# Row copies of a roll in HBM: two DMA rings over the same blocks, or over two halves of the rows

## The chip, the cores and the metric

The kernel runs on one core of one Trainium2 chip. The metric is the device time of one execution in microseconds (us). Times of a kernel are given as the median of several runs with their lowest and highest; a profile is of one execution.

## The reference

A matrix of 8192 x 8192 float32 (256 MiB) is rolled by 100 columns along its rows:

```python
def setup_inputs():
    return {"x": np.random.randn(8192, 8192).astype(np.float32), "shift": 100}

def reference(x, shift):
    return np.roll(x, shift, axis=1)
```

So `out[r, c] = x[r, c - 100]`, and the last 100 columns of x come round to the first 100 of out. Nothing is computed: the kernel moves 268.44 MB from one tensor in HBM to another.

## The kernel before

With n_cols = 8192 and shift 100, `s` is 100, `a` is s rounded up to a multiple of 128, that is 128, and `g = a - s` is 28. Each output row falls into two parts.

The body, columns `a` to 8191 of out, is columns `g` to 8091 of x: 8,064 elements or 32,256 bytes of each row, copied from HBM to HBM with nothing between (lines 31 to 36). `xm` and `om` (lines 31 and 32) view the rows as blocks `c` of 64 rows, each as 16 groups `e` of 4 rows `j`. One DMA takes a fixed `c` and `j` and all 16 `e`: 16 rows, 4 rows (128 KiB) apart. A DMA of 16 rows is spread over 16 DMA engines, one row on each. The loops run over 128 blocks and four `j`; `engines[j % 2]` gives j = 0 and 2 to the queue of SP and j = 1 and 3 to that of ACT, so both queues walk through the same blocks at the same time, on neighbouring rows (32 KiB apart). Each queue issues 256 DMAs. The framework hands out eight completion semaphores to the DMAs of the two queues in turn, four for each queue, and before a DMA reuses a semaphore its queue waits until the DMA that had it has landed. So at most four copies of each queue are under way.

The head, columns 0 to 127 of out, goes through on-chip memory (lines 53 to 75). It is issued by POOL, on a third queue: ten loads into the tiles `t` and `h` (lines 64 to 70; two stages `k` of 4,096 rows), four copies on VectorE that join the pieces from `t` into `h` (lines 68 and 71), and eight stores of 512 bytes per row (line 75). It writes other columns than the body and neither waits for it nor is waited for.

Line 36 is the only line of the body that issues anything:

```python
    if a < n_cols:
        for c in range(n_rows // 64):
            for j in range(4):
                engines[j % 2].dma_start(out=om[c, j, :, a:], in_=xm[c, j, :, g:n_cols - s])
```

Lines 37 to 47 serve other shifts and issue nothing here.

Of the kernel before, what the change touches and what calls it, by code (L numbers as in the profile page):

```python
# [1 line left out]

# [4 lines left out]


@with_exitstack
def kernel(  # L10
    ctx: ExitStack,
    tc: tile.TileContext,
    x: bass.AP,
    shift: int,
    out: bass.AP,
):
    nc = tc.nc
    n_rows, n_cols = x.shape
    s = shift % n_cols
    a = -(-s // 128) * 128  # L20
    g = a - s
    P = nc.NUM_PARTITIONS
    engines = [nc.sync, nc.scalar]
    n_chunks = 16
    rows = n_rows // n_chunks

    xm = x.rearrange("(c e j) w -> c j e w", e=16, j=4)
    om = out.rearrange("(c e j) w -> c j e w", e=16, j=4)
    if a < n_cols:
        for c in range(n_rows // 64):
            for j in range(4):
                engines[j % 2].dma_start(out=om[c, j, :, a:], in_=xm[c, j, :, g:n_cols - s])
    if a == 0:
        return


    if a > 512:
        for i in range(n_chunks):
            r = slice(i * rows, (i + 1) * rows)
            nc.gpsimd.dma_start(out=out[r, :s], in_=x[r, n_cols - s:])
            if g > 0:
                nc.gpsimd.dma_start(out=out[r, s:a], in_=x[r, :g])
        return

    Q, J = 4, 8
    n_st = n_rows // (P * Q * J)
    reads = ctx.enter_context(tc.tile_pool(name="reads", bufs=n_st))
    heads = ctx.enter_context(tc.tile_pool(name="heads", bufs=n_st))
    xt = x.rearrange("(k p j q) c -> k q p j c", q=Q, j=J, p=P)
    ot = out.rearrange("(k p j q) c -> k q p j c", q=Q, j=J, p=P)
    tiles = []
    for k in range(n_st):  # L60
        t = reads.tile([P, Q - 1, J, a], x.dtype)
        h = heads.tile([P, Q, J, a], x.dtype)
        for q in range(1, Q):
            lead = bass.AP(tensor=x.tensor, offset=(k * P * J * Q + q) * n_cols - s,
                           ap=[[J * Q * n_cols, P], [Q * n_cols, J], [1, a]])
            nc.gpsimd.dma_start(out=t[:, q - 1], in_=lead)  # L66
        nc.gpsimd.dma_start(out=h[:, Q - 1, :, :s], in_=xt[k, Q - 1, :, :, n_cols - s:])  # L67
        nc.vector.tensor_copy(h[:, :Q - 1, :, :s], t[:, :, :, :s])  # L68
        if g > 0:
            nc.gpsimd.dma_start(out=h[:, 0, :, s:], in_=xt[k, 0, :, :, :g])  # L70
            nc.vector.tensor_copy(h[:, 1:, :, s:], t[:, :, :, s:])  # L71
        tiles.append(h)
    for k, h in enumerate(tiles):
        for q in range(Q):
            nc.gpsimd.dma_start(out=ot[k, q, :, :, :a], in_=h[:, q])  # L75


# [1 line left out]
_INS = ['x', 'shift']  # L79
_OUTS = [((8192, 8192), 'float32')]  # L80

_NUMBERS = {'shift': 100}


# [26 lines left out]
```

## Time and profile before

| What | Value |
|---|---|
| median of 6 runs | 829.52 us (828.35 to 831.01) |
| the profiled execution | 830.07 us |
| its span, first to last instruction | 828.3 us |
| VectorE busy | 3.7 us |
| POOL busy | 16.1 us |
| POOL's stores (line 75), issue to landing, median | 97.5 us |
| one DMA issue on SP / ACT (line 36), median | 0.510 / 0.517 us |
| first and last issue of line 36 on SP | 0.7 / 815.1 us |

The profile cuts the span into 40 equal slices of 20.7 us and gives for each the mean busy share of the 16 DMA engines in tenths and the GB/s that they moved. A byte that goes from HBM to HBM is counted once in these GB/s, and twice (read and written) in the line on HBM. A line of the queues gives packets, MB and the time that the packets took as a share of what 16 engines had in the span; "software" is POOL's queue, "hardware" those of SP and ACT. A line of the issues gives output and input, the queue, the number of DMAs, KB each and the median us from issue to landing.

### The profile page before, as it was taken

What the parts mean: (1) busy time and instruction counts of PE and PEld (TensorE: products, weight loads), DVE (VectorE), ACT (ScalarE), POOL (GpSimd) and SP (SyncE); (2) the same over time, 40 slices, a digit from 0 to 9 for tenths busy, and PEclk for the clock granted to TensorE, in tenths of its full rate; (3) what the DMA queues carried; (4) which work ended last, traced back from release to release, by engine and by line L of the source; (5) the groups of instructions that cost most, each with busy time, mean ns of one, the idle gap of its engine ahead of it and who ended that gap; (6) DMA issues with size and microseconds to landing.
All of it is one profiled execution on the core that took longest, in us unless ns stands there. A gap on an engine that the chain in (4) does not pass through costs nothing. (4 is left out here: it accounts for less than half of the span.)

```text
span 828.3 us, 589 instructions
## 1 busy us (share of the span) xinstructions
DVE 3.7 (0%) x4; POOL 16.1 (2%) x22
## 2 busy tenths in 40 slices
DVE  0000000000000000000000000000000000000000
POOL 3001001000000000000000000000000000000000
DMA  9999999999999999999999999999999999999998
GB/s 296 324 338 340 339 335 352 344 337 352 345 336 336 326 322 327 327 326 330 321 332 327 335 329 324 327 332 321 324 338 316 334 337 322 329 330 329 333 326 271
DMA packets 18724, 272.70 MB, mean 329 GB/s; under 512 B 8480, under 2 KB 8480, under 8 KB 10528
## 3 DMA queue, kind: packets, MB, share of 16 engines
q1 hardware_dynamic: 8192, 132.14, 47.9%
q10 hardware_dynamic: 8192, 132.14, 47.2%
q0 software_dynamic: 2336, 8.39, 3.9%
q14 instruction: 4, 0.03, 0.0%
HBM read 268.44 MB, written 268.44 MB: 648 GB/s over the span
## 5 line engine op out<-in xcount | busy, mean ns | idle before, releaser
L75 POOL DMA_DIRECT2D out_dram<-h x8 | 6.9, 957 | 92.4 <-DMA h<-in_x_dram 81.2
L66 POOL DMA_DIRECT2D t<-in_x_dram x6 | 5.4, 912 | 0.8 <-PEq L106 0.8
L68 DVE COPY h<-t 128x2400 f32<-128x2400 f32 x2 | 2.8, 1410 | 117.5 <-DMA t<-in_x_dram 117.5
L67 POOL DMA_DIRECT2D h<-in_x_dram x2 | 1.8, 884 | 16.5 <-DMA t<-in_x_dram 16.5
L70 POOL DMA_DIRECT2D h<-in_x_dram x2 | 1.8, 884 | 13.6 <-DMA t<-in_x_dram 13.6
L71 DVE COPY h<-t 128x672 f32<-128x672 f32 x2 | 1.0, 504 | 0.0
L92 POOL MEMSET const-float32-0.0<- 128x1 f32 x1 | 0.1, 100 | 0.2 <-issue 0.2
L92 POOL MEMSET const-bfloat16-1.0<- 128x1 bf16 x1 | 0.1, 103 | 0.0
L92 POOL MEMSET const-float32-1.0<- 128x1 f32 x1 | 0.1, 100 | 0.0
L92 POOL MEMSET const-uint8-127<- 128x1 uint8 x1 | 0.1, 100 | 0.0
## 6 DMA issues: line engine op xcount, KB each, us to landing
out_dram<-in_x_dram ACTq DMA_DIRECT2D x256, 504.0 KB, 12.7
out_dram<-in_x_dram SPq DMA_DIRECT2D x256, 504.0 KB, 12.7
out_dram<-h POOLq DMA_DIRECT2D x8, 512.0 KB, 97.5
t<-in_x_dram POOLq DMA_DIRECT2D x6, 512.0 KB, 67.8
h<-in_x_dram POOLq DMA_DIRECT2D x2, 400.0 KB, 85.1
h<-in_x_dram POOLq DMA_DIRECT2D x2, 112.0 KB, 82.7
```

What stands on the lines that cost most here:

```text
L66: nc.gpsimd.dma_start(out=t[:, q - 1], in_=lead)
L67: nc.gpsimd.dma_start(out=h[:, Q - 1, :, :s], in_=xt[k, Q - 1, :, :, n_cols - s:])
L68: nc.vector.tensor_copy(h[:, :Q - 1, :, :s], t[:, :, :, :s])
L70: nc.gpsimd.dma_start(out=h[:, 0, :, s:], in_=xt[k, 0, :, :, :g])
L71: nc.vector.tensor_copy(h[:, 1:, :, s:], t[:, :, :, s:])
L75: nc.gpsimd.dma_start(out=ot[k, q, :, :, :a], in_=h[:, q])
L92: nc = _bacc.Bacc("TRN2", target_bir_lowering=False, num_devices=1)
```

## The change

The body's loop runs over half as many blocks, and in each step issues two DMAs: SP copies row `j` of each group of block `c`, ACT the same of block `c + 64`. SP goes through rows 0 to 4095 and ACT through rows 4096 to 8191. Each queue issues 256 DMAs of 16 rows, in the order SP, ACT, SP, ACT; the shape of a DMA, the bytes and the rest of the kernel stay.

```diff
     if a < n_cols:
-        for c in range(n_rows // 64):
+        half = n_rows // 64 // 2
+        for c in range(half):
             for j in range(4):
-                engines[j % 2].dma_start(out=om[c, j, :, a:], in_=xm[c, j, :, g:n_cols - s])
+                for q, eng in enumerate(engines):
+                    eng.dma_start(out=om[q * half + c, j, :, a:], in_=xm[q * half + c, j, :, g:n_cols - s])
```

## The prediction

> **What bounds the kernel now.** I read the page of the profiled execution first: its span, the slices, the queues and the HBM line.
>
> ```profile
> span 828.3 us, 589 instructions
> ...
> DMA  9999999999999999999999999999999999999998
> GB/s 296 324 338 340 339 335 352 344 337 352 345 336 336 326 322 327 327 326 330 321 332 327 335 329 324 327 332 321 324 338 316 334 337 322 329 330 329 333 326 271
> DMA packets 18724, 272.70 MB, mean 329 GB/s; under 512 B 8480, under 2 KB 8480, under 8 KB 10528
> ...
> q1 hardware_dynamic: 8192, 132.14, 47.9%
> q10 hardware_dynamic: 8192, 132.14, 47.2%
> q0 software_dynamic: 2336, 8.39, 3.9%
> ...
> HBM read 268.44 MB, written 268.44 MB: 648 GB/s over the span
> ```
>
> The reader is to see that the 16 DMA engines are busy from the first slice to the last, nearly all of it with the two hardware rings (q1 and q10, those of SP and ACT), and that the engine's other work (POOL's queue, q0) takes 3.9%. Each ring has 8,192 packets: 4,096 rows of 32,256 bytes (132.14 MB / 4,096) and as many 4-byte completion writes. So each engine carries 8,192 / 16 = 512 rows.
>
> Next, the issues and the waits of the queues, to see whether issuing limits anything.
>
> ```profile
> out_dram<-in_x_dram ACTq DMA_DIRECT2D x256, 504.0 KB, 12.7
> out_dram<-in_x_dram SPq DMA_DIRECT2D x256, 504.0 KB, 12.7
> ```
>
> ```profile
> SPq L36 <- DMA out_dram<-in_x_dram: 679.7, 252, 3.9
> ```
>
> SP issued 256 copies and before 252 of them it waited for an older copy to land, 679.7 us in all: four copies are in flight per ring, and the queue idles for lack of landings, not the other way round. An issue takes 0.51 us (the records of line 36), so 256 of them need 131 us of 828. The count agrees: 8 copies in flight x 516,096 bytes / 12.7 us = 325 GB/s, the rate of the slices. The chain of waits is of no use here: it follows POOL and stops 139 us into the span, while the end is set by the last row copies, issued at 815 us.
>
> Last, the stretch in which the two rings are alone (POOL's last packet starts at about 256 us; the stretch is 289.9 to 807.6 us, slices 15 to 39).
>
> ```profile
> DMA packets 10530, 169.77 MB, mean 328 GB/s; under 512 B 5266, under 2 KB 5266, under 8 KB 5266
> ...
> q1 hardware_dynamic: 5266, 84.94, 51.1%
> q10 hardware_dynamic: 5262, 84.81, 48.6%
> ```
>
> Half of the 10,528 ring packets are rows: 5,264 rows in 517.7 us on 16 engines, 1,574 ns for each row and its completion write (9 ns by the packet records). The records of single packets show what those 1,574 ns are made of. The shortest row took 1,192 ns (27.1 GB/s on one engine), 1,579 of the 8,192 rows took under 1,200 ns, the median is 1,485, the mean 1,529, and one in ten is over 1,941. The floor is so sharp that I read it as an engine's own pace, and the excess, 1,529 - 1,192 = 337 ns a row, as waiting for memory that 16 engines read and write at once. That the floor is the engine's and the excess the memory's is inference; that excess exists is read off.
>
> **The change, part by part.** The sum before, per engine: rings 47.9% + 47.2% = 95.1% of 828.3 = 787.7 us; POOL's queue 3.9% = 32.3 us; together 820.0 us; the other 8.3 us are the edges (the first and last slices, 296 and 271 GB/s) and gaps. Around the span lie 830.07 - 828.3 = 1.8 us. The profiled execution's 830.07 us is 0.55 above the median of 829.52, so I add differences to the median.
>
> Copies issued: 256 on SP and 256 on ACT, each 16 rows by 8,064 elements, before and after. Removed 0, added 0. The built program has the same rows of instructions on every engine, the same four copies in flight per ring, and the waits stand before the same copies. Price 0, since count and durations (0.51 us per issue, hidden under 679.7 us of waiting) don't change; if that cover were gone the issue would still need only 131 us beside 788 us of transfers. POOL's 18 DMAs and VectorE's four copies (3.7 us) are untouched; they had 550 us to spare before, so a later landing of theirs delays nothing. No wait is added.
>
> What moves is which row a ring is at. Before, one engine meets rows 4e, 4e+1, 4e+2, 4e+3 of a block by turns from the two rings: 32 KiB apart, all in one 128 KiB piece, and the 16 engines walk a window of a few MiB together. After, the SP ring gives it row 4e + j of block c, and the ACT ring row 4e + j of block c + 64: 4,096 rows, exactly 128 MiB, further. Both windows are then walked at once, in x and in out. The trace of before shows no pair of row copies that far apart, so its cost is bounded from rows nearby.
>
> The near rows are the slices with the rings alone, in which relative positions of the 16 engines drift: mean 327.9 GB/s, slowest 316, fastest 338. If all ring time ran at the slowest, 787.7 x (327.9/316 - 1) = +29.7 us; at the fastest, 787.7 x (327.9/338 - 1) = -23.5 us. The far row is the excess itself: doubled, 512 x 337 ns = +173 us; gone, -173 us. A gain near that far end I exclude, because these bytes would then pass at 537 / 655 us = 820 GB/s, while no slice of this execution with rings alone moved above 2 x 338 = 676 GB/s to and from HBM.
>
> I take a loss and put it halfway between no effect and the slowest slice: 29.7 / 2 = +14.9 us, so 829.5 + 14.9 = **844 us**. The reason for the sign: an engine overlaps the write of one row with the read of the next (inference: the rows follow each other back to back while their writes need to land). Before, these two rows are neighbours, 32 KiB apart in their tensors; after, they sit at the same place in windows a power of two apart, where the same banks of memory are likelier to be asked for two different lines. The reason for a small size: only one of an engine's neighbours changes, whereas the 16 engines still stand on 16 different rows, 128 KiB apart. It is nearer to the slices than to the doubled excess, since the rings alternate on one engine and never run in step side by side.
>
> A rule of the Trainium skill speaks against this change. In the trace, POOL's descriptors, which step far through x among the ring rows in the first 250 us, don't harm these: the third slice to the thirteenth read 335 to 352 GB/s, POOL's own bytes included. DMA: Bandwidth & Descriptors, "Latency and other measured facts", tells that copies whose partitions lie megabytes apart at a power of two lose up to half their rate (pitch of 512 KiB 207 GB/s, of 4 MiB 103). By that rule at its worst the ring time would double, to some 1,600 us; by the trace's POOL rows it would not move. I take neither as it stands: the page's streams run in step on many partitions, and POOL's pieces are 512 bytes.
>
> A second page bounds a gain. The trace's HBM line shows 648 GB/s. HBM Reference, "Specifications (TRN2)", gives about 716 GB/s per domain; by it the sum could not fall below 537 MB / 716 GB/s = 750 us, an estimate.
>
> **The rivals.**
>
> *No difference.* The rings' addresses don't matter because 16 engines, drifted against each other, already spread over the memory, and the rate is a ceiling of read and write traffic together. For it: slices with the rings alone stay within 4% of 328 for 500 us whatever the engines' drift, and each engine does the same work. Against it: one row takes from 1,192 to over 1,941 ns, so something in the pattern decides. It gives 829.5 us, and it includes the case that the change does not do what it says: the instruction stream is the same, so if memory places both halves alike nothing is left of it.
>
> *Faster, through less crowding.* One mechanism: at present all 16 engines and both rings stand in one window of a few MiB, and rows of neighbouring addresses queue for the same lines of memory; two windows spread them. Its place is the excess of 337 ns a row. For it: only one row in five runs at the floor. Against it: the two rings have to share the same memory rate afterwards, and slices above 335 are rare. At the fastest slice's rate it gives 829.5 - 23.5 = 806 us, at half of that gain 818 us. It decides from where the gain in waiting, per row, passes what the 128 MiB pairing costs (15 us / 512 = 29 ns by my figure); with less than that my forecast's sign stands.
>
> *Strong aliasing.* The windows fall on the same banks and the excess rises by over a third. A third is 512 x 112 ns = +57.5 us, 887 us; doubled it is 829.5 + 173 = 1,002 us. For it: the distance is an exact power of two in both tensors. Against it: x and out, equal in size, are probably placed a whole tensor apart, so such pairs of a read and a write exist already.
>
> **How the numbers follow.** Slower by up to a third of the excess: 0.48, and 844 us as its value. Strong aliasing: 0.10. No difference (within 0.2%, 1.7 us, which is what a measurement of this kernel can tell): 0.12. Faster: 0.30. So faster 0.30, same 0.12, slower 0.58. The range runs from the fastest slice's 806 us to the 888 us where strong aliasing begins; beyond lie that rival's 0.10 and, below, some 0.06 of the faster case. The likeliest case's own range is 831.5 to 888.
>
> **What would show it.** If I am right: the slices with the rings alone fall to about 322 GB/s in the mean (327.9 x 787.7 / 802.6), the DMA row stays at 9 throughout, the landing time of a copy rises from 12.7 to about 12.9 us, fewer rows take under 1,200 ns, the SP queue's wait rises by about the 15 us that the span grows, and POOL's busy time is unchanged. If the faster rival holds: slices of 333 to 338, landing near 12.4 us, more rows at the floor. If there is no difference, mean and spread of the slices stay. I would be wrong in the step on issue if a DMA slice fell below 9 in the middle, or if the SP queue's wait fell by more than the span; wrong in the sign if the mean row took under 1,529 ns; and wrong in size alone if the rate dropped below 305 GB/s with busy engines.

## The result and the profile after

The changed kernel takes 833.3 us in the median of 16 runs (830.0 to 835.01), the kernel before 829.31 us in 35 runs beside it (826.34 to 831.54): a ratio of 1.0047, 95% interval 1.0036 to 1.0057, or 3.9 us more (829.31 x 0.0047). The sign is the forecast's; the size is a quarter of the forecast 14.9 us.

The page of the changed kernel, in the order of the lines shown of before (span, slices, queues, HBM, issues):

```profile
span 829.8 us, 589 instructions
...
DMA  9999999999999999999999999999999999999997
GB/s 298 345 342 332 327 344 349 331 344 353 345 349 321 327 334 327 333 325 330 327 331 331 316 328 323 325 330 325 333 325 328 327 327 327 337 328 327 323 320 252
...
q10 hardware_dynamic: 8192, 132.14, 48.1%
q1 hardware_dynamic: 8192, 132.14, 46.9%
q0 software_dynamic: 2336, 8.39, 4.0%
...
HBM read 268.44 MB, written 268.44 MB: 647 GB/s over the span
...
out_dram<-in_x_dram ACTq DMA_DIRECT2D x256, 504.0 KB, 12.8
out_dram<-in_x_dram SPq DMA_DIRECT2D x256, 504.0 KB, 12.8
```

The reader is to see that nothing has changed its kind: the same packets, the same number of issues, DMA engines busy throughout. The rings' shares make (48.1% + 46.9%) x 829.8 = 788.3 us an engine, against 787.7 before; POOL's 33.2 against 32.3; the rest 8.3 in both. This profiled execution took 831.54 us, the second shortest of the 16, and the one of before 830.07, so between the two pages stand 1.5 of the 3.9 us, and a share rounded to a tenth of a per cent is good to 0.4 us. The waits of SP's queue and the stretch with the rings alone (289.9 to 807.6 us) of the changed kernel:

```profile
SPq L39 <- DMA out_dram<-in_x_dram: 681.7, 252, 4.7
```

```profile
DMA packets 10513, 169.51 MB, mean 327 GB/s; under 512 B 5257, under 2 KB 5257, under 8 KB 5257
...
q10 hardware_dynamic: 5254, 84.78, 50.1%
q1 hardware_dynamic: 5257, 84.71, 49.5%
```

SP waits 2.0 us longer for landings, and 10,511 ring packets fit where 10,528 did. Both point to slower rows; but in two single executions that differ by less than the runs of one kernel do (830.0 to 835.0), they can't carry an explanation. What follows rests on ratios from repeated runs.

### The profile page after: what moved, and what is told of

Its sections match the earlier page's. It is cut to its first block, busy times and chain, and to the rows that moved or that the text cites. A ratio compares the mean times of both kernels' runs of the same rounds, so it can differ in the third digit from the quotient of the medians.

```text
span 829.8 us, 589 instructions
## 1 busy us (share of the span) xinstructions
DVE 3.7 (0%) x4; POOL 16.1 (2%) x22
## 2 busy tenths in 40 slices
DMA packets 18724, 272.70 MB, mean 329 GB/s; under 512 B 8480, under 2 KB 8480, under 8 KB 10528
## 3 DMA queue, kind: packets, MB, share of 16 engines
q10 hardware_dynamic: 8192, 132.14, 48.1%
q1 hardware_dynamic: 8192, 132.14, 46.9%
## 6 DMA issues: line engine op xcount, KB each, us to landing
out_dram<-in_x_dram ACTq DMA_DIRECT2D x256, 504.0 KB, 12.8
out_dram<-in_x_dram SPq DMA_DIRECT2D x256, 504.0 KB, 12.8
```

## The experiments

All of them move all rows with 512 copies of 16 rows, and what is changed is which row follows which. Where a kernel changes something else as well (which rows one copy takes, which queue issues it, where the rows are written), the text says so. "Row number" means j, the place of a row in its group of four, each row 32 KiB after the one before. One ring's rows and the other's come to an engine by turns: a row of each ring, then both completion writes. The packet records don't name the engine, but their times show it: with the rings alone, 92% of ACT's rows in the kernel before and 84% in the changed kernel start within 5 ns of the end of a row of SP, and 96% and 95% of SP's rows within 5 ns of the end of a completion write of ACT. So an order can be written as the row numbers that one engine meets: before 0 1 2 3, after 0 0 1 1 2 2 3 3. Ratios are to the kernel before on the same chip; that kernel took 820.4 to 821.2 us in the first four groups (on three chips) and 828.8 us in the last one (on a fourth), so times are compared inside a group only. The ratios are not quotients of the medians given beside them, and lie up to 0.0016 above or 0.0007 below these.

### Distance or row number

The changed kernel again, with the block and the row of a copy named `b` and `r` (after_again); the edits below are against it where nothing else is said:

> The changed kernel once more, as the measure for its neighbours on the same chip. All theories: 1.0047 of the kernel before, within 0.001.

Measured 1.0058 (1.0045 to 1.0071), 824.33 us against 820.39.

With ACT's rows turned by two (half_rows_turned):

```diff
-                    b, r = q * half + c, j
+                    b, r = q * half + c, (j + 2 * q) % 4
```

> As the changed kernel, but ACT takes the four rows of a group in the order 2, 3, 0, 1, so the two rings stand 128 MiB plus or minus 64 KiB apart. Theory A (the exact power of two makes the two rings' rows ask for the same banks; 64 KiB is enough to leave them): about 1.000, 829 us. Theory B (two windows far apart cost, whatever their exact distance): 1.0047, 833 us.

Measured 1.0004 (0.9994 to 1.0013): the loss is gone, with the rings still 128 MiB apart, give or take 64 KiB.

With ACT's blocks turned (half_blocks_turned):

```diff
-                    b, r = q * half + c, j
+                    b, r = q * half + (c + 21 * q) % half, j
```

> As the changed kernel, but ACT begins its half 21 blocks further on and comes round to them at the end: 170 MiB, later 42 MiB apart, no power of two. Theory A with banks chosen by higher bits of the address: about 1.000, 829 us. Theory B: 1.0047, 833 us.

Measured 1.0091 (1.0076 to 1.0106). No power of two in the distance, and no less loss.

SP the even blocks, ACT the odd ones (alternate_blocks):

```diff
-                    b, r = q * half + c, j
+                    b, r = 2 * c + q, j
```

> SP copies the even blocks and ACT the odd ones, all four rows of each: the rings stand 2 MiB apart, in one window. Theory B: about 1.000, 829 us, since the window stays one. Theory C (not the distance, but that an engine no longer gets neighbouring rows from the two rings in turn): 1.0047, 833 us. Theory A: between the two, as 2 MiB is a power of two as well.

Measured 1.0084 (1.0068 to 1.01). The rings are 2 MiB apart, in one window, and the loss is there. So theory B falls by two of these kernels, and theory A's large power of two by half_blocks_turned. Theory C, that an engine needs neighbouring rows from the two rings, falls by half_rows_turned, whose order 0 2 1 3 has none. Against after_again (up to 1.0071), the two kernels with the larger loss differ by some 0.3%; the interval of alternate_blocks overlaps its own, that of half_blocks_turned (from 1.0076) does not. That part isn't explained.

The same turn in the near arrangement (alternate_blocks_turned, against alternate_blocks):

```diff
-                    b, r = 2 * c + q, j
+                    b, r = 2 * c + q, (j + 2 * q) % 4
```

> SP the even blocks, ACT the odd ones, 2 MiB apart, but ACT takes the four rows of a group in the order 2, 3, 0, 1. Theory D (what costs is that the two rings are at the same row number j of their groups of four, that is, at addresses that agree in the bits of 32 and 64 KiB; distance is of no account): 1.000, against 1.0084 without the turn. Theory B (distance): 1.008 again.

Measured 1.0011 (0.9996 to 1.0026). At 2 MiB as at 128 MiB the loss comes and goes with the row numbers alone. The traces show it in the stretch with the rings alone (289.9 to 807.6 us); first alternate_blocks:

```profile
q10 hardware_dynamic: 5275, 85.10, 52.5%
q1 hardware_dynamic: 5273, 85.07, 47.2%
```

and half_rows_turned, of the same group:

```profile
q1 hardware_dynamic: 5335, 86.01, 50.4%
q10 hardware_dynamic: 5333, 86.04, 49.2%
```

Half of the packets are rows, so 5,274 against 5,334 rows in 517.7 us on 16 engines: 1,571 and 1,553 ns a row, its completion write included. The 18 ns make 512 x 18 = 9 us of an execution; the two profiled executions lie 7.3 us apart (826.74 and 819.45), the medians 6.2. The engines are busy in both, and the rows themselves take longer: 1,557 against 1,539 ns in the mean of that stretch's packet records.

### How far apart in row numbers

Groups of eight rows, SP rows 0 to 3, ACT rows 4 to 7 (eights):

```diff
-        half = n_rows // 64 // 2
-        for c in range(half):
+        xm = x.rearrange("(c e j) w -> c j e w", e=16, j=8)
+        om = out.rearrange("(c e j) w -> c j e w", e=16, j=8)
+        for c in range(n_rows // 128):
...
-                    b, r = q * half + c, j
+                    b, r = c, j + 4 * q
```

> Groups of eight rows per engine in blocks of 128 rows; SP takes rows 0 to 3 and ACT rows 4 to 7 of each group, so the rings are 128 KiB apart with the same j modulo 4. Theory D with the bits of 32 and 64 KiB alone: 1.005 or more. Theory D with the bit of 128 KiB counting too: 1.000 to 1.002. The engines stand 256 KiB apart here, which is a change of its own.

Measured 1.0 (0.9988 to 1.0012). No loss 128 KiB apart, with row numbers that agree modulo 4, so agreement in the bits of 32 and 64 KiB alone does not bring the loss here. But a copy's 16 rows lie 256 KiB apart in this kernel instead of 128, a change of its own that no run separates.

### One engine's sequence, or the crowd of engines

Two blocks for each row number, ACT turned by two, order 0 2 0 2 1 3 1 3 (two_row_numbers), and the same without the turn, order 0 0 0 0 1 1 1 1 (one_row_number):

```diff
-        for c in range(half):
-            for j in range(4):
+        for c in range(0, half, 2):
+            for i in range(8):
                 for q, eng in enumerate(engines):
-                    b, r = q * half + c, j
+                    b, r = q * half + c + i % 2, (i // 2 + 2 * q) % 4
```

> Halves as in the changed kernel; SP takes row j of a block and row j of the next before it goes on to j + 1, and ACT the same, two row numbers ahead. An engine's successive rows then always differ in j, but over four successive rows only two row numbers occur (in the kernel before all four do). Theory D1 (engines crowd each other: what counts is how many row numbers the 16 engines are on at one time, and they lie about four rows apart): 1.005 as the changed kernel, or more. Theory D2 (one engine's write of a row meets its own read of the next): 1.000.

Measured 0.9995 (0.9981 to 1.001): two row numbers at one time are harmless when they are two apart. Theory D1, the crowd of engines, had 1.005 or more here.

> As two_row_numbers, but ACT at the same row number as SP: four successive rows of an engine have one j. The suspected cost is doubled. Theory D1: clearly above 1.006, some 1.012 or more, as one row number is shared where the changed kernel shares two. Theory D2: 1.012 as well, since now all steps of an engine, not every second one, go to the same j. Theory B: 1.005, as the changed kernel.

Measured 1.0039 (1.0025 to 1.0054). Three of four successive steps stay at one row number, where the changed kernel has every second, and the loss is no larger. A price per equal pair does not fit; both theories had 1.012.

ACT one row number ahead, order 0 1 1 2 2 3 3 0 (turned_by_1), and three ahead, order 0 3 1 0 2 1 3 2 (turned_by_3):

```diff
-                    b, r = q * half + c, j
+                    b, r = q * half + c, (j + 1 * q) % 4
```

> Halves, with ACT one row number ahead of SP (j + 1 modulo 4). On an engine the packets mostly come as pairs, a row of each ring, then both completion writes, then the next pair. Theory D2 (any two successive rows of an engine): if SP's row leads the pair, ACT's row and SP's next one share their row number across the completion writes, which costs: 1.003 to 1.005; if ACT's leads, 1.000. Theory E (only the two rows of a pair meet, the completion writes keep pairs apart): 1.000 whichever ring leads.

Measured 1.0079 (1.0062 to 1.0097).

> Halves, with ACT three row numbers ahead of SP, that is one behind. Theory D2: the mirror of turned_by_1, 1.003 to 1.005 if ACT's row leads the pair and 1.000 if SP's does, so that one of the two kernels is slow. Theory E: 1.000.

Measured 0.9985 (0.9974 to 0.9997). No equal numbers follow each other here, but in turned_by_1 they do, SP's next row after ACT's. Equal numbers across the completion writes seem to cost as much as within a pair, against theory E; but the turns are less regular in turned_by_1 (51% of ACT's rows start at the end of a row of SP), so equal numbers may stand within pairs as well, and the single ring below decides it.

All copies on SP, in the order of before (one_ring_neighbours) and of after (one_ring_halves):

```diff
-                engines[j % 2].dma_start(out=om[c, j, :, a:], in_=xm[c, j, :, g:n_cols - s])
+                nc.sync.dma_start(out=om[c, j, :, a:], in_=xm[c, j, :, g:n_cols - s])
```

This is one_ring_neighbours, against the kernel before; one_ring_halves has the changed kernel's loops with `nc.sync` in place of `eng`.

> All 512 row copies from SP alone, eight under way, in the order of the kernel before (blocks in turn, j 0 to 3). A measure for one_ring_halves. Issuing needs 512 x 0.51 = 261 us and stays hidden; if a completion write after every row holds the engine up, it is slower than the kernel before by up to 512 x 0.1 us = 51 us; otherwise within 1.01.

Measured 1.0018 (1.0006 to 1.0031).

> All 512 row copies from SP alone, in the order of the changed kernel: row j of a block, then row j of the block 64 further, then j + 1. Theory E: the completion write now stands between the two rows, so they no longer meet: equal to one_ring_neighbours within 0.002. Theory D2: slower than one_ring_neighbours by about 0.005.

Measured 1.0103 (1.0086 to 1.0121): 828.3 us against 822.03 with the same single ring. Two rings are not needed for the loss. A completion write stands between the rows here (97% of the rows start within 5 ns of the end of one), and equal row numbers on both sides of it cost all the same, so theory E falls. The stretch 289.9 to 807.6 us of one_ring_neighbours:

```profile
q1 hardware_dynamic: 10644, 171.69, 99.9%
```

and of one_ring_halves:

```profile
q1 hardware_dynamic: 10526, 169.78, 99.9%
```

One queue keeps the 16 engines at 99.9% in both; with the order of after, 1.1% fewer rows pass. That is the effect of the order with the second ring taken away, somewhat larger than with it (0.76% by the medians against 0.5% for the changed kernel in the two groups).

### Reads, writes, or a write and the next read

Here ACT's rows, and in the last kernel SP's too, are read and written under different row numbers, so that the rows of a group come out in another order than the reference's:

```diff
-                    b, r = q * half + c, j
-                    eng.dma_start(out=om[b, r, :, a:], in_=xm[b, r, :, g:n_cols - s])
+                    b, r, w = q * half + c, j, (j + 2 * q) % 4
+                    eng.dma_start(out=om[b, w, :, a:], in_=xm[b, r, :, g:n_cols - s])
```

This is reads_together; writes_together exchanges r and w, and write_meets_read has `r = (j + 2 * q) % 4` and `w = (j + 2 - 2 * q) % 4`.

> Halves; both rings read row j, but ACT writes what it read to row j + 2 (modulo 4) of its group, so in the second half the rows of a group come out in another order. Equal row numbers remain for read and next read, and for a write and the next read at SP to ACT; none between successive writes. If the reads or write-to-read meetings cost: 1.005 to 1.008. If only write and write cost: 1.000.

Measured 1.0014 (1.0001 to 1.0027).

> Halves; ACT reads row j + 2 (modulo 4) and writes it to row j, so its rows come out in another order. Equal row numbers remain between successive writes only. If write and write cost: 1.005 to 1.008. If reads, or a write and the next read: 1.000.

Measured 1.0028 (1.0009 to 1.0047).

> Halves; SP reads row j and writes it to row j + 2, ACT reads row j + 2 and writes it to row j (modulo 4), so the rows of all groups come out in another order. Successive reads differ and successive writes differ, but SP's write has the row number of ACT's next read. If the meeting of a write and the next read costs: 1.005 to 1.008. If reads among themselves or writes among themselves: 1.000.

Measured 1.0 (0.999 to 1.001). SP's write under the row number of ACT's next read costs nothing. Equal reads (in reads_together, beside such a meeting) and equal writes (in writes_together, alone) both stay below the 1.005 that the expectations had for a single cause. Each seems to carry a part, and 0.0014 + 0.0028 = 0.0042 is near the changed kernel's loss, but the intervals are too wide to call that sum shown.

### Dwelling at one row number

The row number outside, all blocks for one j before the next (row_number_outside):

```diff
-        for c in range(half):
-            for j in range(4):
+        for j in range(4):
+            for c in range(half):
```

> Halves as in the changed kernel, but the loop over the row number stands outside: all blocks with j = 0 first, then j = 1, and so on. All successive rows of an engine now have the same row number. Theory D2 with a price per equal pair: at least twice the changed kernel's loss, 1.010 or more. Theory G (equal numbers cost nothing by themselves; the slow orders are those where an engine dwells for two rows and then steps on): 1.000 to 1.004.

Measured 0.9968 (0.9957 to 0.998), 817.95 us against 820.55: every successive row has the same row number, and the kernel has the lowest ratio of all, below both kernels of this study. A price per equal pair falls for good. One thing more differs here: SP runs a copy ahead of ACT (its last issue comes at 803.1 us, ACT's at 806.5, where the kernel before has 815.1 and 815.3), so the rows that meet are mostly 126 MiB apart, not 128. What this is worth was not measured. Its page (span and queues):

```profile
span 816.3 us, 589 instructions
...
q1 hardware_dynamic: 8192, 132.14, 47.5%
q10 hardware_dynamic: 8192, 132.14, 47.4%
```

The rings take 94.9% of 816.3 = 774.7 us an engine, for the same bytes. This is not to be held against the 787.7 us of the page before, which was taken where that kernel took 829.3 us; in this group it took 820.55, and what the order gained is the 2.6 us between the medians.

The same with ACT turned by two, order 0 2 0 2 throughout (row_number_outside_turned, against row_number_outside):

```diff
-                    b, r = q * half + c, j
+                    b, r = q * half + c, (j + 2 * q) % 4
```

> As row_number_outside, but ACT is always two row numbers ahead, so no two successive rows of an engine share one. Theory H (equal pairs cost as in the changed kernel, and a separate gain hides it): 0.985 to 0.992. Theory G (equal pairs cost nothing by themselves): 0.995 to 1.001.

Measured 1.0007 (0.9995 to 1.0019). The turn that helps the changed kernel brings no gain here, and theory H falls. That it takes away the gain of row_number_outside is read across two chips, since that kernel was not run on this one.

Four blocks for each row number (one_row_number_8, against one_row_number), order eight times 0, eight times 1:

```diff
-                    b, r = q * half + c + i % 2, i // 2
+                    b, r = q * half + c + i % 4, i // 4
```

with `i` to 16 and `c` in steps of four.

> Halves, both rings at the same row number for eight rows of an engine (four blocks each), then the next row number. Theory H: at least 1.004, as one_row_number, for there are more equal pairs. Theory G, with a price that falls as the dwell grows (two rows 1.005 to 1.009, four rows 1.004, 128 rows 0.997): about 1.000.

Measured 0.9994 (0.9984 to 1.0005). With both rings at the same row number, in halves, the price falls with the length of the dwell, the number of successive rows of an engine at one row number: two rows 1.0047 and 1.0058 (the changed kernel, twice), four rows 1.0039, eight rows 0.9994, 128 rows (64 of each ring) 0.9968. The ratios come from several groups, and the interval of four rows (1.0025 to 1.0054) overlaps those of two; the fall from four rows to eight, and to 128, is clear of the intervals. In one_row_number_8 the rings stay in step (94% of ACT's landings come 0.15 to 0.23 us from one of SP's copy of the same number), so rows exactly 128 MiB apart follow each other in it, and nothing is lost: the power of two alone does not bring the loss.

## Why the prediction was right or wrong

*What bounds the kernel* held: the DMA row stays at 9 until the last slice, and SP waits 681.7 us for landings. The rows' own pace decides; one ring alone, with half as many issuing queues, keeps the engines at 99.9%. The shortest row took 1,192 ns in the packet records of every kernel, so the orders change what a row takes above that; that this excess is waiting for memory stays the prediction's inference. One reading there was mixed: the mean of 1,529 ns is that of all 8,192 rows, while the rows of the stretch with the rings alone, from which the 1,574 ns come, took 1,560 ns in the mean and those before it 1,469. The excess with the rings alone was 368 ns, not 337.

*Removed 0, added 0* held: 256 issues per queue, POOL's busy time 16.1 us in both, no slice in the middle below 9.

*The sign* came out as forecast, but in part by luck, for the step that gave it failed. It said that an engine's write of one row and its read of the next collide because both stand at the same place in windows a power of two apart. The power of two is not needed (half_blocks_turned loses 0.9% at 170 and 42 MiB), nor are the far windows (alternate_blocks loses 0.8% at 2 MiB), nor do they suffice (half_rows_turned loses nothing at 128 MiB), nor does the exact power of two (one_row_number_8, 0.9994), and the meeting of a write and the next read costs nothing (write_meets_read 1.0000). What stands of the step is its first half: the row that follows on the same engine is what changed, and one_ring_halves shows that this order alone costs 0.76% (828.3 / 822.03). What the runs showed in place of the collision: the loss goes with the row numbers of successive rows on an engine, and with how long they stay equal.

*The size*, halfway to the slowest slice, was the step that mis-sized the sum: +14.9 us against a measured 3.9. The slices do not measure order. Those with the rings alone spread from 316 to 338 GB/s before and from 316 to 337 after, with means of 327.9 and 327.5: the spread is there in each kernel and averages out, and half of its lower side is no price for an order. The forecast mean of 322 did not come; landing went from 12.7 to 12.8 us instead of 12.9, SP's wait rose by 2.0 us instead of 15. The mean row rose from 1,529 to 1,531 ns, and 1,488 rows instead of 1,579 took under 1,200 ns, so these signs pointed the right way, in two single executions.

*No difference* had the better size. Its argument, that the rings' addresses don't matter because the engines' drift spreads them anyway, fits the distance of the windows, which is of no account in the pair half_rows_turned and before, and fails for the row numbers. The drift itself was not tested.

*Faster, through less crowding*: spreading the rings over two windows gains nothing (half_rows_turned 1.0004). A gain exists, but in an order that stays at one row number for 128 rows.

*Strong aliasing* is excluded for this pattern: the largest ratio of any order was 1.0103, some 7 us by the medians (828.3 against 821.18). The Trainium skill's page DMA: Bandwidth & Descriptors, section "Latency and other measured facts", gives losses of up to a half for copies whose row pitch is a large power of two. The runs here, with rows 128 MiB apart on two rings, show 0.5%, and none at all in half_rows_turned (1.0004) or one_row_number_8 (0.9994).

What stays open is why. The landing records show the 16 engines finishing one copy over 5.5 us before and 6.2 to 6.3 us in the changed kernel (medians over 512 copies, from the first engine to the last), some four rows of 1.57 us. A dwell of two or four rows is then no longer than the engines' spread, and they may stand on two neighbouring row numbers at a time, while a dwell of 128 puts nearly all of them on one; this is argued, not shown. It fits the dwell series, but not by itself the orders 0 1 2 3 and 0 2 1 3, which mix row numbers too and lose nothing against each other. Nor does the spread sort the kernels: it is 5.6 us in alternate_blocks, which loses 0.8%, and 7.1 us both in turned_by_1, which loses 0.8%, and in turned_by_3, which loses nothing. How the memory places addresses was not measured, and no run separates the crowd of engines from the sequence on one.

## What to carry to other kernels

When a copy between two tensors in HBM keeps all DMA engines busy, the order in which one engine gets its rows can be worth up to about one per cent (here 0.997 to 1.010 over the 16 kernels that write the reference's result). One queue instead of two cost 0.2% here (1.0018), and moving the queues from 2 to 128 MiB apart nothing that was clear of the intervals; 170 and 42 MiB (half_blocks_turned) cost 0.3% more than 128, which isn't explained. Test a suspected address pattern by turning one coordinate at a time, near and far, before believing in a distance. The spread between slices of one execution is not the price of a pattern, and differences below 1% are read from repeated runs, not from two pages.

## What the runs showed of the hardware that had not been expected

- One ring with eight copies under way does nearly as well as two with four each, 1.0018 (1.0006 to 1.0031), though every row is followed by its own completion write; the records show 9 ns for such a write.
- Going through all blocks at one row number, with 2 MiB between a ring's successive rows, is faster than taking neighbouring rows: 0.9968 (0.9957 to 0.998). With ACT two row numbers ahead it is not: 1.0007 (0.9995 to 1.0019).
- The same program of the kernel before took 820.4 to 821.2 us in four groups of runs on three chips and 828.8 us on a fourth, and 829.3 us beside the result: 1% between chips or sessions, twice the effect that was studied.
